# Row sums of a 16384 x 1024 matrix: the last group's loads in other sizes, and another moment for the first store

## The chip, the cores and the metric

The kernel runs on one core of a Trainium2 chip. The metric is the device time of one execution in microseconds (us), the median of several executions. A profile of one execution comes with it: its span starts with the first load that SyncE issues and ends with the closing work of the program.

## The reference

The input x has 32 x 512 rows of 1024 float32 numbers (67.1 MB). The output is the sum of each row.

```python
def reference(x):          # x: (32, 512, 1024) float32
    return np.sum(x, axis=-1).astype(np.float32)
```

## The kernel before

The 16384 rows are cut into 8 groups of 2048. In a group each of the 128 partitions holds 16 consecutive rows (`BIG = 16`), so one group is 8 MB, and 64 KB in each partition. A group lies in a tile `t` of a pool with three buffers; the sums of all rows gather in one tile `sums` of 128 x 128 numbers, 16 columns for each group.

All loads are issued by SyncE, in the order of the program (lines 137 and 179). A load of a group waits until VectorE has read the group that used its buffer before. The order of the work on each engine is that of the program text.

Three helpers add up rows:

- `vec` (line 98) is one VectorE reduction over several rows.
- `act` (line 125) is one ScalarE copy of one row with an accumulated output; its copy goes to a PSUM tile `unread` that nobody reads.
- `halves` (line 112) is a custom VectorE instruction for one row or a part of one: it adds the second half of its input to the first half, element by element, and accumulates the sums. An instruction that reads the accumulator out follows it.

`rows` (line 134) loads `n` rows for each partition and sums them: the first `n - n_act` by `vec`, the last `n_act` by `act`, one after the other.

Groups 0 to 5 are summed by VectorE alone (group 0 is loaded as 4 and 12 rows), group 6 half by each engine. The last group, number 7, is loaded in pieces of 8, 4, 2 and 1 rows, of which ScalarE sums 4, 2, 1 and 1. Its last row comes in three column pieces of 482, 288 and 254 (`pieces`, line 87; loads at line 179). The three lie one behind the other in the tile, but a free column is left before the third and one after it. The sums of the first two pieces are accumulated into these two free columns, and the third `halves` adds up piece and both columns: `whole`, 256 columns.

There are two stores (line 145). The one of groups 0 to 6 (56 KB) is issued by ScalarE's queue, behind its activations, and it is held until the sum over the first piece is done (`front`, line 186). The one of group 7 (8 KB) is issued by SyncE after the last sum. The closing work of the program (reported at line 214) waits for both.

`order_waits` sets the order in which an instruction with several waits makes them.

Of the kernel before, what the change touches and what calls it, by code (L numbers as in the profile page):

```python
# [58 lines left out]
@with_exitstack  # L59
def kernel(  # L60
    ctx: ExitStack,
    tc: tile.TileContext,
    x: bass.AP,
    out: bass.AP,
):
    nc = tc.nc
    nc.at_finalize(issue_first_load_at_entry)
    nc.at_finalize(order_waits)
    fp32 = mybir.dt.float32
    P = 128  # L70
    batch, seq, dim = x.shape
    rows = batch * seq
    J = rows // P
    BIG = 16


    x_g = x.flatten_outer_dims().rearrange("(g p j) d -> g p j d", p=P, j=BIG)
    out_v = out.rearrange("b s -> (b s)").rearrange("(g p j) -> p g j", p=P, j=BIG)

    def rows_from(j, n):  # L80
        return x_g[j // BIG, :, j % BIG : j % BIG + n, :]

    last = J // BIG - 1
    FIRST = 4
    pieces = (482, 288, 254)

    with (
        tc.tile_pool(name="in", bufs=3) as inpool,  # L90
        tc.tile_pool(name="unread", bufs=4, space=bass.MemoryType.PSUM) as upool,
        tc.tile_pool(name="stage", bufs=1) as stpool,
        tc.manual_schedule(),
    ):
        sums = stpool.tile([P, J], fp32)

        def vec(dst, src):
            return nc.vector.tensor_reduce(  # L98
                out=dst, in_=src, axis=mybir.AxisListType.X, op=mybir.AluOpType.add
            )  # L100

        def hold(inst, until, reason):
            tc.add_manual_dep(
                inst.ins,
                until.ins.name,
                mybir.DependencyInfo(mybir.DependencyClass.Sync, mybir.DependencyReason.DATA),
                reason=reason,
            )

        def halves(dst, src):  # L110
            n = src.shape[-1] // 2
            return nc.vector.tensor_tensor_reduce(  # L112
                out=src[:, :n],
                in0=src[:, :n],
                in1=src[:, n:],
                scale=1.0,
                scalar=0.0,
                op0=mybir.AluOpType.add,
                op1=mybir.AluOpType.add,
                accum_out=dst,  # L120
            )

        def act(dst, src, n):
            unread = upool.tile([P, dim], fp32)
            nc.scalar.activation(  # L125
                out=unread[:, :n],
                in_=src,
                func=mybir.ActivationFunctionType.Copy,
                accum_out=dst,
            )  # L130

        sums_of = []

        def rows(t, a, n, j, n_act):
            nv = n - n_act
            block = t[:, a * dim : (a + n) * dim].rearrange("p (n d) -> p n d", d=dim)
            load = nc.sync.dma_start(out=block, in_=rows_from(j, n))  # L137
            if nv:
                sums_of.append(vec(sums[:, j : j + nv], block[:, :nv, :]))
            for q in range(nv, n):  # L140
                act(sums[:, j + q : j + q + 1], block[:, q, :], dim)
            return load

        def store(eng, g0, g1):
            return eng.dma_start(
                out=out_v[:, g0:g1],
                in_=sums[:, g0 * BIG : g1 * BIG].rearrange("p (g j) -> p g j", j=BIG),
            )

        for g in range(last):  # L150
            t = inpool.tile([P, BIG * dim + 4], fp32)
            if g == 0:
                rows(t, 0, FIRST, 0, 0)
                first = sums_of[-1]
                rows(t, FIRST, BIG - FIRST, FIRST, 0)
                continue
            load = rows(t, 0, BIG, g * BIG, BIG // 2 if g == last - 1 else 0)
            if g == 1:
                hold(load, first, "no descriptors of later loads while the first ones start")

        t = inpool.tile([P, BIG * dim + 4], fp32)
        a = 0
        j = last * BIG
        for n, n_act in ((8, 4), (4, 2), (2, 1), (1, 1)):
            rows(t, a, n, j + a, n_act)
            a += n

        j += a
        at = a * dim
        c = 0
        parts = []
        for width in pieces:
            if len(parts) == len(pieces) - 1:
                at += 1
            part = t[:, at : at + width]
            nc.sync.dma_start(out=part, in_=rows_from(j, 1)[:, 0, c : c + width])
            parts.append(part)  # L180
            at += width
            c += width
        whole = t[:, at - width - 1 : at + 1]
        front = halves(whole[:, :1], parts[0])
        halves(whole[:, width + 1 :], parts[1])
        hold(store(nc.scalar, 0, last), front, "its packets come behind those of the loads")
        halves(sums[:, j : j + 1], whole)
        store(nc.sync, last, last + 1)

# [29 lines left out]
```

## Time and profile before

| | |
|---|---|
| median of 4 runs | 163.01 us (162.18 to 163.09) |
| the profiled execution: time | 163.05 us |
| the profiled execution: span | 161.3 us |
| VectorE (DVE) busy | 121.1 us, 75% |
| ScalarE (ACT) busy | 18.5 us, 11% |
| GpSimd (POOL) busy | 0.2 us |
| HBM read over the span | 67.11 MB, 417 GB/s |

In the lines of the profile, PE, DVE, ACT, POOL and SP are TensorE, VectorE, ScalarE, GpSimd and SyncE; a q behind a name is the queue of the engine that issues its instructions. L98 is line 98 of the kernel. `out<-in` names the tile written and the tile read. In a timeline each line has its start and length in us, the engine, the line, the operation and, in brackets, how long the engine had been idle and what ended that. The chain of work that ended last is followed back from the last instruction, at each step to what released it.

### The profile page before, as it was taken

To read this page: it belongs to the slowest core of one execution; us is meant where nothing else is said; L and a number is where in the kernel's file an instruction comes from. 1 tells how busy PE (TensorE), PEld (TensorE's weight loads), DVE (VectorE), ACT (ScalarE), POOL (GpSimd) and SP (SyncE) were. 2 spreads that over 40 slices of the span, in tenths; PEclk is the share of its full clock that TensorE was granted. 3 is DMA by queue.
4 is the path that set the end of the run, shared out by engine and by line. 5 is a ranking of instruction groups with operands and counts; after the bars stand their busy time and mean duration, and the time that the engine had idled before them with its cause. 6 is when DMAs were issued, how large, how long until landed. Compare 5 with 4: busy or idle time off the path is not lost.

```text
span 161.3 us, 125 instructions
## 1 busy us (share of the span) xinstructions
DVE 121.1 (75%) x17; ACT 18.5 (11%) x33; POOL 0.2 (0%) x4
## 2 busy tenths in 40 slices
DVE  0280069960899949999399994999949998597982
ACT  3000000000000000000000000000000000596882
POOL 0000000000000000000000000000000000000000
DMA  7999995996996996979959959959969959999992
GB/s 264 451 524 451 390 520 260 520 520 260 520 520 260 520 520 260 520 309 471 520 260 520 520 260 520 520 260 520 520 260 520 520 260 520 390 390 451 402 400 63
DMA packets 3216, 67.18 MB, mean 417 GB/s; under 512 B 1296, under 2 KB 1680, under 8 KB 1808
## 3 DMA queue, kind: packets, MB, share of 16 engines
q1 hardware_dynamic: 2304, 67.12, 97.4%
q10 hardware_dynamic: 912, 0.06, 0.3%
HBM read 67.11 MB, written 0.07 MB: 417 GB/s over the span
## 4 chain that ended last, share of the span: by engine, by line
DMA 73%; DVE 25%; SPq 1%; issue 0%; DVEq 0%
DMA t<-in_x_dram 73%; DVE sums L98 24%; SPq L137 1%; DVE t L112 1%; DVEq L112 0%; DVEq L214 0%
## 5 line engine op out<-in xcount | busy, mean ns | idle before, releaser
L98 DVE TENSOR_REDUCE sums<-t 128x16 f32<-128x16384 f32 (+5 forms) x11 | 120.1, 10917 | 36.9 <-DMA t<-in_x_dram 36.9
L125 ACT ACTIVATE unread<-t 128x1024 f32<-128x1024 f32 x16 | 16.2, 1013 | 139.0 <-DMA t<-in_x_dram 138.9
L125 ACT ACTIVATION_READ_ACCUMULATOR unread<-t 128x1 f32 x16 | 3.0, 187 | 0.0
L112 DVE CUSTOM_DVE_ANT_0 t<-t 128x241 f32<-128x241 f32 (+2 forms) x3 | 1.0, 338 | 0.9 <-DMA t<-in_x_dram 0.8
L125 ACT ACT_TABLE_LOAD x1 | 1.3, 1283 | 0.8 <-PEq L203 0.8
L112 DVE DVE_READ_ACCUMULATOR2_ANT t<- 128x1 f32 x2 | 0.2, 82 | 0.0
L203 POOL MEMSET const-bfloat16-1.0<- 128x1 bf16 x1 | 0.1, 102 | 0.0
L203 POOL MEMSET const-uint8-127<- 128x1 uint8 x1 | 0.1, 102 | 0.0
L203 POOL MEMSET const-float32-0.0<- 128x1 f32 x1 | 0.1, 99 | 0.2 <-issue 0.2
L203 POOL MEMSET const-float32-1.0<- 128x1 f32 x1 | 0.1, 99 | 0.0
L112 DVE DVE_READ_ACCUMULATOR2_ANT sums<- 128x1 f32 x1 | 0.1, 83 | 0.0
## 6 DMA issues: line engine op xcount, KB each, us to landing
t<-in_x_dram SPq DMA_DIRECT2D x1, 6144.0 KB, 20.9
t<-in_x_dram SPq DMA_DIRECT2D x2, 2048.0 KB, 21.4
t<-in_x_dram SPq DMA_DIRECT2D x1, 4096.0 KB, 31.2
t<-in_x_dram SPq DMA_DIRECT2D x1, 1024.0 KB, 37.7
t<-in_x_dram SPq DMA_DIRECT2D x1, 512.0 KB, 38.5
t<-in_x_dram SPq DMA_DIRECT2D x1, 241.0 KB, 38.7
t<-in_x_dram SPq DMA_DIRECT2D x1, 144.0 KB, 38.6
t<-in_x_dram SPq DMA_DIRECT2D x1, 127.0 KB, 38.4
```

The costliest lines, as they stand in the source:

```text
L98: return nc.vector.tensor_reduce(out=dst, in_=src, axis=mybir.AxisListType.X, op=mybir.AluOpType.add)
L112: return nc.vector.tensor_tensor_reduce(out=src[:, :n], in0=src[:, :n], in1=src[:, n:], scale=1.0, scalar=0.0, op0=mybir.AluOpType.add, op ...
L125: nc.scalar.activation(out=unread[:, :n], in_=src, func=mybir.ActivationFunctionType.Copy, accum_out=dst,)
L137: load = nc.sync.dma_start(out=block, in_=rows_from(j, n))
L203: nc = _bacc.Bacc("TRN2", target_bir_lowering=False, num_devices=1)
```

## The change

The last group is loaded as 8, 5 and 2 rows and then a last row in two column pieces of 560 and 464; before it was 8, 4, 2 and 1 rows and a last row in three pieces. ScalarE sums 4, 2 and 1 rows of the three row loads. In the pieces of 5 and 2 rows, VectorE's rows (3 and 1) are no longer summed by one `vec` but by one `halves` for each row. The second column piece of the last row has one free column ahead of it, which takes the sum of the first piece, and one behind it, which VectorE fills with zero, so that `whole` has an even number of columns (466). The store of groups 0 to 6 is held until the last `halves` of the two-row piece is done, instead of the sum over the first column piece.

```diff
-    pieces = (482, 288, 254)
+    pieces = (560, 464)
...
-        def rows(t, a, n, j, n_act):
+        def rows(t, a, n, j, n_act, pairs=False):
             nv = n - n_act
             block = t[:, a * dim : (a + n) * dim].rearrange("p (n d) -> p n d", d=dim)
             load = nc.sync.dma_start(out=block, in_=rows_from(j, n))
-            if nv:
+            if pairs:
+                for q in range(nv):
+                    sums_of.append(halves(sums[:, j + q : j + q + 1], block[:, q, :]))
+            else:
                 sums_of.append(vec(sums[:, j : j + nv], block[:, :nv, :]))
...
-        a = 0
         j = last * BIG
-        for n, n_act in ((8, 4), (4, 2), (2, 1), (1, 1)):
-            rows(t, a, n, j + a, n_act)
-            a += n
-
+        rows(t, 0, 8, j, 4)
+        rows(t, 8, 5, j + 8, 2, pairs=True)
+        rows(t, 13, 2, j + 13, 1, pairs=True)
+        a = BIG - 1
...
-        at = a * dim
-        c = 0
-        parts = []
-        for width in pieces:
-            if len(parts) == len(pieces) - 1:
-                at += 1
-            part = t[:, at : at + width]
-            nc.sync.dma_start(out=part, in_=rows_from(j, 1)[:, 0, c : c + width])
-            parts.append(part)
-            at += width
-            c += width
-        whole = t[:, at - width - 1 : at + 1]
-        front = halves(whole[:, :1], parts[0])
-        halves(whole[:, width + 1 :], parts[1])
-        hold(store(nc.scalar, 0, last), front, "its packets come behind those of the loads")
+        c, width = pieces
+        whole = t[:, a * dim + c : BIG * dim + 2]
+        nc.vector.memset(whole[:, width + 1 :], 0.0)
+        part = t[:, a * dim : a * dim + c]
+        nc.sync.dma_start(out=part, in_=rows_from(j, 1)[:, 0, :c])
+        nc.sync.dma_start(out=whole[:, 1 : width + 1], in_=rows_from(j, 1)[:, 0, c:])
+        hold(store(nc.scalar, 0, last), sums_of[-1], "its packets come behind those of the loads")
+        halves(whole[:, :1], part)
         halves(sums[:, j : j + 1], whole)
         store(nc.sync, last, last + 1)
```

## The prediction

> **What bounds the kernel now.** I read the page's chain first, then the chain in order of time, then the timeline of the last 13 us, then the busy time by stretches around the end. The chain says who ends last:
>
> ```profile
> DMA t<-in_x_dram 73%; DVE sums L98 24%; SPq L137 1%; DVE t L112 1%; DVEq L112 0%; DVEq L214 0%
> ```
>
> The loads of x are 73% of it, and the 24% of the reductions at line 98 are no second bound: they are stretches in which the chain walks through the reduction that frees a buffer while loads go on beside it (page: 417 GB/s mean over the span). The change lies in the last group only, so its price is read from the end of the chain (start, length, what; all in us):
>
> ```profile
> 119.03 38.72 DMA t<-in_x_dram
> 157.74 0.02 issue
> 157.77 0.69 DVE t L112 x4
> 158.46 0.03 issue
> 158.49 0.02 DVEq L112
> 158.51 0.08 issue
> 158.59 0.29 DVE t L112
> ```
>
> At 157.74 the first piece of the last row has landed. From there VectorE is the chain: two sums over pieces (0.69 with their accumulator reads), then 0.13 in which the third sum waits for the results of the first two, because it reads them, then the third sum, 0.29. The timeline gives landings (an instruction that had waited for a load starts 0.02 after it) and the two stores:
>
> ```profile
> 148.41 4.42 DVE L98 TENSOR_REDUCE sums<-t 128x4 f32<-128x4096 f32 x1 [1.03 <-DMA t<-in_x_dram]
> 153.30 2.29 DVE L98 TENSOR_REDUCE sums<-t 128x2 f32<-128x2048 f32 x1 [0.47 <-DMA t<-in_x_dram]
> 155.79 1.22 DVE L98 TENSOR_REDUCE sums<-t 128x1 f32<-128x1024 f32 x1 [0.20 <-DMA t<-in_x_dram]
> 157.08 1.03 ACT L125 ACTIVATE unread<-t 128x1024 f32<-128x1024 f32 x1
> 158.22 0.42 ACTq L145 DMA_DIRECT2D out_dram<-sums  x1
> 158.92 0.35 SPq L145 DMA_DIRECT2D out_dram<-sums  x1
> ```
>
> The pieces of 8, 4, 2 and 1 rows landed at 148.39, 153.28, 155.77 and 157.06. VectorE stood idle before each (the brackets), so it keeps up with the loads until the last row. The table of DMA issues puts the last piece (127 KB) at 38.4 after an issue at 120.0, so at 158.4, and the stores' landings at 2.1 after 158.22 (160.3) and 1.6 after 158.92 (160.5). The second ends the program; 0.8 of closing work follows it to 161.3. The profiled execution took 163.05: its span plus 1.75 around it. It lies 0.04 above the median of the four runs, 163.01.
>
> **The loads.** Seven loads become five. The four-row piece took 153.28 - 148.39 = 4.89, or 1.22 a row, the two-row piece 2.49, the single row 1.29. Five rows at 1.22 are 6.11, so they land at 154.50, and two rows at 2.49 land at 156.99, where the single row landed at 157.06: 0.07 earlier. If the fifth row keeps the price of the single row (1.29), the gain is nothing. The last row took 158.4 - 157.06 = 1.34 in three pieces and would take 1.29 or a little less as one; for two I take the middle, 1.31. The last landing is then 156.99 + 1.31 = 158.30, with 158.25 and 158.40 as ends. The first of two pieces, 560 columns, has 482 of them priced by the old first piece, 157.74 - 157.06 = 0.68; scaled by 560/482 that is 0.79, so it lands at 157.78.
>
> Against this stands a rule. The Trainium skill, page DMA: Bandwidth & Descriptors, section Anatomy of one DMA, gives each transfer a fixed 2.0 us beside its bytes (fitted on the GpSimd path, while these loads come from SP); two transfers fewer would by that be an estimated 4 us. The trace disagrees: the three pieces land within 1.34 together, so a transfer's fixed part lies beside the others' bytes, and the sum above stands.
>
> SP issues all of these around 117 to 120.5, when 38 us of transfers are queued ahead, so two issues fewer (0.48 each at most) bring nothing. No queue is moved past by them.
>
> **VectorE.** The three sums over halves took 411, 310 and 294 ns for 241, 144 and 128 elements: 160 ns and 1.04 ns for an element. So a whole row (512 elements) is 693, the 560-column piece (280) 452, and the last one (466 columns with the two added ones, 233 elements) 403. One starts 0.05 before its forerunner ends (157.77 + 0.41 against 158.13).
>
> - Eight-row piece: as before, 4.42.
> - Five-row piece, three paired rows: 154.52 + 3 x 0.65 = 156.5, half a microsecond ahead of the next landing. Where the cover is gone (each would have to wait 0.13 as the third sum does), it is 156.9, still before 157.01.
> - Two-row piece: row 13 runs 157.01 to 157.70. Before, ScalarE had this time alone; VectorE waited 0.75. The next instruction may start at 157.66.
> - The new zero fill of one column stands behind it in VectorE's queue. No such fill is in the trace on VectorE; GpSimd's four take 0.10, an accumulator read on VectorE 0.08, and the longest that I allow is a sum's fixed 0.16 with the wait of 0.13. I take 0.10, nearest in kind, so to 157.76: hidden, as the first piece lands at 157.78. At 0.29 it would push the chain by 0.15. Below nothing it can't go, since it is added.
> - First piece: 157.80 to 158.25, accumulator read out at 158.26. The last sum reads that result, so the 0.14 between the read (end 158.45) and the third sum (158.59) stays: 158.40. Its data are there at 158.30, so VectorE, not the load, is last here.
> - Last sum: 158.40 + 0.40 = 158.80, against 158.88 before.
>
> So one link of three in the closing chain goes, but the links that stay are longer and the first comes after a row's sum. Net: 0.08 earlier. With the load's worst end (158.40 + 0.02) it is 0.06; with the slow fill 0.07 later than before.
>
> **ScalarE and the stores.** ScalarE takes seven rows of the group instead of eight; its last one starts at 157.01 instead of 157.08 and ends at 158.16 instead of 158.23. SP's last store waits for that too, hidden by 0.64 of VectorE's work. The store of the first seven groups waited for the first piece (158.18, issued at 158.22). Now it waits for row 13, done at 157.72, and stands on ScalarE's queue behind the last activation. Which of the two holds it the trace doesn't show: 157.75 if the queue runs ahead of the engine, 158.18 if not. Nothing else is queued behind it. Its landing at 2.1 comes to 159.85 or 160.28, before the last store's in both cases, so this step is worth nothing on the path, or up to 0.1 if the last store meets fewer of its packets. Does it hurt the loads? The stretches show (length, busy of the engines, clock, DMA share, GB/s):
>
> ```profile
> 148.40:153.20 4.80, 4.42 (x1) 4.27 (x8) 0.00 (x0) 1.00 0.98 420
> 153.20:155.60 2.40, 2.29 (x1) 2.19 (x4) 0.00 (x0) 1.00 0.97 408
> ...
> 156.60:157.60 1.00, 0.41 (x1) 0.86 (x3) 0.00 (x0) 1.00 1.05 361
> 157.60:158.00 0.40, 0.23 (x1) 0.40 (x1) 0.00 (x0) 1.00 0.44 147
> 158.00:159.00 1.00, 0.75 (x6) 0.23 (x2) 0.00 (x0) 1.00 0.00 0
> 159.00:159.40 0.40, 0.00 (x0) 0.00 (x0) 0.00 (x0) 1.00 0.45 45
> 159.40:160.00 0.60, 0.00 (x0) 0.00 (x0) 0.00 (x0) 1.00 0.77 79
> ```
>
> The loads' bytes end before 158.0, and the stores' bytes begin after 159.0, some 0.8 to 0.9 behind the issue at 158.22. Issued at 157.75, they begin at 158.55 at the earliest: still behind the loads.
>
> **Sum.** 163.05 - 0.08 = 162.97 for the profiled execution; by the median, 163.01 - 0.08 = 162.93, so 162.9. The last store still lands 1.6 after its issue at 158.84.
>
> **The rivals.**
> 1. *The loads gain more.* The rate falls from 420 GB/s in the stretch of the four-row piece to 361 where the single row and the pieces run, and the two-row piece's stretch has 408. If the single row (0.52 MB) moves from 361 to 408, that is 1.45 - 1.29 = 0.16, everything behind it comes earlier, and with up to 0.1 from the last store the time is about 162.7. Against it: the single row's landing came only 1.29 after its forerunner.
> 2. *VectorE becomes later.* The fill and a wait in front of the first piece cost 0.29 and row 13 starts late (157.08): the last sum starts at 158.6 or 158.7 and is longer by 0.11, so 163.1 to 163.2. For it speaks that row 13's sum is new in the last microsecond.
> 3. *Slower: the store's packets get in between the last loads.* Place: the 16 DMA engines at 157 to 158. Price: the stores keep them busy 0.45 x 0.40 + 0.77 x 0.60 = 0.64 in the stretches above, and if all of that goes before the last piece the time is 163.01 - 0.08 + 0.64 = 163.6. It decides from an issue some 0.85 before the loads' last byte, so before about 157.1; the wait for row 13 (157.72) speaks against it, unless the store follows something that is ready sooner than I read. The Trainium skill (same page, section Queues, rings and completion order) says that an engine alternates between queues packet by packet, which would make this the cost of every early store; no load and store overlap in this trace.
> 4. *Nothing that counts changes*: the gain of the loads and the longer last sum cancel (the load's worst end and the fill at 0.29 give 163.1), and the four runs spread from 162.18 to 163.09 anyway.
>
> **How the numbers follow.** About 0.5% (0.82 us) is what a measurement of this kernel can tell from no change. Chances: the forecast 0.50 (162.8 to 163.0), rival 1 0.18, rival 2 0.13, rival 3 0.07, rival 4 0.12. No step that I priced reaches 0.82 in either direction. Faster by more than that needs rival 1 together with a median at the low end of the spread of runs (162.18 is at the line): 0.14. Slower needs rival 3 with its price above the sum, or a wait that the trace doesn't show: 0.09. The rest, 0.77, is within. The range runs from the lowest run of before, 162.2, to rival 2 with half of rival 3, 163.4.
>
> **What would show it.** In the changed profile: the two-row piece's sums start at 157.0; three paired rows of 0.69 end before that; the last sum starts 0.14 behind an accumulator read, not 0.02 behind a landing; SP's store is issued at 158.8 to 158.9; no store bytes before 158.5. I am wrong if the last load lands after 158.5, if the store's bytes appear beside load bytes, if a paired row takes clearly over 0.7, or if the time moves by over 0.5 in either direction.

## The result, and the profile after

The changed kernel takes 162.13 us (median of 54 runs, 161.86 to 162.75), the kernel before, measured with it, 162.51 us (78 runs, 162.10 to 163.12). The ratio is 0.9981, 95% interval 0.9974 to 0.9988: faster by 0.31 us, or 0.20 to 0.42 by the interval, and so within 0.5%. The means, 162.23 and 162.54, differ by that 0.31; the medians lie 0.38 apart, the fastest runs 0.24. The profiled execution took 162.01 with a span of 160.2.

The spans of the two profiled executions differ by 1.04, far more than that. Where the difference lies is seen from the eight-row piece of the last group: its sums start at 148.41 before and at 147.56 after, so 0.85 of it had come up ahead of anything that was changed. It was complete at the sums of group 4 (99.98 against 99.13), long before SyncE issued the first load of the last group (117.2 and 116.4). In the fourteen profiles of this study that start lies between 147.43 and 148.41, as far apart as the runs of one kernel. I therefore call it the mark, and count from it. The landings and ends of spans below are the trace's own time stamps, which the profile's tables round to 0.1; the times of the stores' packets (a packet is one piece of a transfer on one DMA engine) are from the trace's packet records.

The chain of the changed kernel in order of time, its end (start, length, what):

```profile
118.23 39.34 DMA t<-in_x_dram
157.57 0.04 issue
157.62 0.40 DVE t L112
```

The chain now goes over from the loads to VectorE with one sum left, instead of three with a wait in between. The timeline shows what is around it:

```profile
147.56 4.42 DVE L98 TENSOR_REDUCE sums<-t 128x4 f32<-128x4096 f32 x1 [1.03 <-DMA t<-in_x_dram]
153.78 0.69 DVE L112 CUSTOM_DVE_ANT_0 t<-t 128x512 f32<-128x512 f32 x1 [1.80 <-DMA t<-in_x_dram]
156.29 1.03 ACT L125 ACTIVATE unread<-t 128x1024 f32<-128x1024 f32 x1 [0.32 <-DMA t<-in_x_dram]
156.29 0.69 DVE L112 CUSTOM_DVE_ANT_0 t<-t 128x512 f32<-128x512 f32 x1 [0.59 <-DMA t<-in_x_dram]
156.94 0.06 DVE L176 MEMSET t<- 128x1 f32 x1
157.01 0.45 DVE L112 CUSTOM_DVE_ANT_0 t<-t 128x280 f32<-128x280 f32 x1
157.02 0.41 ACTq L148 DMA_DIRECT2D out_dram<-sums  x1
157.39 0.08 DVE L112 DVE_READ_ACCUMULATOR2_ANT t<- 128x1 f32 x1
157.62 0.40 DVE L112 CUSTOM_DVE_ANT_0 t<-t 128x233 f32<-128x233 f32 x1
158.05 0.35 SPq L148 DMA_DIRECT2D out_dram<-sums  x1
```

The last sum ends 10.46 after the mark; before, it ended at 10.47. The closing chain of loads and sums is in this profile no shorter at all. What is shorter stands in the table of DMA issues, as the time from issue to landing of the two stores (KB, us). The first two lines are the changed kernel's, the third is the last store of the kernel before; the first store has 2.1 there too:

```profile
out_dram<-sums ACTq DMA_DIRECT2D x1, 56.0 KB, 2.1
out_dram<-sums SPq DMA_DIRECT2D x1, 8.0 KB, 1.4
out_dram<-sums SPq DMA_DIRECT2D x1, 8.0 KB, 1.6
```

The last store landed 1.6 after its issue before, and 1.4 now. The stretches of the changed kernel say why (length, busy of DVE, ACT, POOL, clock, DMA share, GB/s):

```profile
157.40:157.80 0.40, 0.26 (x3) 0.04 (x1) 0.00 (x0) 1.00 0.00 0
157.80:158.20 0.40, 0.23 (x2) 0.00 (x0) 0.00 (x0) 1.00 0.46 46
158.20:158.60 0.40, 0.00 (x0) 0.00 (x0) 0.00 (x0) 1.00 0.81 85
158.60:158.80 0.20, 0.00 (x0) 0.00 (x0) 0.00 (x0) 1.00 0.29 26
158.80:159.20 0.40, 0.00 (x0) 0.00 (x0) 0.00 (x0) 1.00 0.23 21
```

The first store's bytes begin to move at 157.98, as VectorE ends its last sum, and go on while the last store is only being issued (158.05). They are through at 158.72, and the last store has the engines to itself. In the kernel before the two ran into each other: the first store's packets moved from 159.18 to 159.95, those of the last one from 159.77 to 160.01. The queues' packets in the stretch around the last store's show it (queue: packets, MB, share of 16 engines; q10 is ScalarE's queue, q1 SyncE's). The first two lines are the kernel before, 159.70 to 160.10, the third is the changed kernel, 158.72 to 159.20, where q10 has none:

```profile
q10 hardware_dynamic: 233, 0.01, 34.5%
q1 hardware_dynamic: 144, 0.01, 21.8%
q1 hardware_dynamic: 144, 0.01, 19.3%
```

### The profile page after: what moved, and what is told of

It is laid out like the page before. It is cut to its first block, busy times and chain, and to the rows that moved or that the text cites. A ratio compares the mean times of both kernels' runs of the same rounds, so it can differ in the third digit from the quotient of the medians.

```text
span 160.2 us, 126 instructions
## 1 busy us (share of the span) xinstructions
DVE 120.1 (75%) x22; ACT 17.3 (11%) x31; POOL 0.2 (0%) x4
## 4 chain that ended last, share of the span: by engine, by line
DMA 73%; DVE 25%; SPq 1%; issue 0%; DVEq 0%
DMA t<-in_x_dram 73%; DVE sums L98 24%; SPq L137 1%; SPq L178 0%; DVE t L112 0%; DVEq L209 0%
## 5 line engine op out<-in xcount | busy, mean ns | idle before, releaser
L98 DVE TENSOR_REDUCE sums<-t 128x16 f32<-128x16384 f32 (+3 forms) x9 | 116.6, 12953 | 35.4 <-DMA t<-in_x_dram 35.4
L125 ACT ACTIVATE unread<-t 128x1024 f32<-128x1024 f32 x15 | 15.2, 1012 | 139.4 <-DMA t<-in_x_dram 139.4
L112 DVE CUSTOM_DVE_ANT_0 t<-t 128x512 f32<-128x512 f32 (+2 forms) x6 | 3.5, 603 | 2.5 <-DMA t<-in_x_dram 2.4
```

Of the source, the lines that this page charges most:

```text
L98: return nc.vector.tensor_reduce(out=dst, in_=src, axis=mybir.AxisListType.X, op=mybir.AluOpType.add)
L112: return nc.vector.tensor_tensor_reduce(out=src[:, :n], in0=src[:, :n], in1=src[:, n:], scale=1.0, scalar=0.0, op0=mybir.AluOpType.add, op ...
L125: nc.scalar.activation(out=unread[:, :n], in_=src, func=mybir.ActivationFunctionType.Copy, accum_out=dst,)
```

## The experiments

Each was timed beside the kernel before. The table gathers what the profiles show from the mark on; the two stores of each kernel are called the first (groups 0 to 6, ScalarE's queue) and the last (group 7, SyncE's queue).

| kernel | first store issued | last sum ends | last store lands | landing less last sum | span ends | ratio (95% interval) |
|---|---|---|---|---|---|---|
| before | 9.81 | 10.47 | 12.11 | 1.64 | 12.86 | 1 |
| changed | 9.46 | 10.46 | 11.92 | 1.46 | 12.67 | 0.9981 (0.9974 to 0.9988) |
| changed, again | 9.35 | 10.36 | 11.81 | 1.45 | 12.56 | 0.9981 (0.9966 to 0.9997) |
| changed, store late | 9.83 | 10.35 | 12.12 | 1.77 | 12.87 | 1.0007 (0.9991 to 1.0023) |
| the same, again | 9.94 | 10.45 | 12.23 | 1.78 | 12.98 | 0.9997 (0.9978 to 1.0016) |
| before, store early | 8.68 | 10.48 | 11.93 | 1.45 | 12.68 | 0.9998 (0.9981 to 1.0014) |
| the same, again | 8.69 | 10.50 | 11.95 | 1.45 | 12.70 | 0.9981 (0.9963 to 0.9998) |

**The changed kernel again**, with no edit.

> The changed kernel itself, once more, as the mark for the others. In the first pair of profiles I count from the start of the sums of the eight-row piece (148.41 before, 147.56 changed), since both kernels are alike up to there: the last sum ended 10.48 later before and 10.46 changed, the last store landed after another 1.63 before and 1.46 changed, and the span ended 12.9 and 12.6 after the mark. All theories expect the same here: last sum 10.45 to 10.50 after the mark, last store landing 1.4 after its issue, time 0.2 to 0.4 us under the kernel before.

The last sum ended at 10.36 instead of 10.46, so this part of the tail differs by 0.1 between executions of one kernel; the last store landed 1.4 after its issue, as before. The ratio, 0.9981, is the same.

**The changed kernel with the old moment of the store**, run twice.

```diff
-        hold(store(nc.scalar, 0, last), sums_of[-1], "its packets come behind those of the loads")
-        halves(whole[:, :1], part)
+        front = halves(whole[:, :1], part)
+        hold(store(nc.scalar, 0, last), front, "its packets come behind those of the loads")
```

> The changed kernel, but the store of groups 0 to 6 follows the sum over the first column piece again. Store theory (the gain comes from the last store, which finds the first store's packets gone): the first store is issued at about 157.5 instead of 157.0, its bytes end at about 159.2 instead of 158.7, the last store lands 1.6 instead of 1.4 after its issue, and 0.15 to 0.2 of the gain of 0.31 goes. Load theory (fewer and larger loads bring the end): time as the changed kernel, 0.3 under the kernel before. VectorE theory (a shorter closing chain): also unchanged.

The gain is gone. The last store's landing in its table of DMA issues:

```profile
out_dram<-sums SPq DMA_DIRECT2D x1, 8.0 KB, 1.7
```

The last sum ended 0.12 earlier than in the kernel before, and the last store still landed at the same 12.1 after the mark: what the sums gave, the store took back. In the stretches the store bytes of this kernel end before 159.8, at 11.6 after the mark, as those of the kernel before do (160.0):

```profile
159.40:159.80 0.40, 0.00 (x0) 0.00 (x0) 0.00 (x0) 1.00 0.74 74
159.80:160.00 0.20, 0.00 (x0) 0.00 (x0) 0.00 (x0) 1.00 0.00 0
```

The first store is issued at the same distance from the mark in both (9.81 and 9.83), and it is this that fixes the end. I expected 0.15 to 0.2 of the gain to go; the two runs, 1.0007 and 0.9997 (mean 1.0002), leave nothing of it. The second was expected so:

> The changed kernel with the store after the first column piece, once more (first 1.0007, interval 0.9991 to 1.0023): the new loads and sums without the new moment of the store. If the first store's packets set the end, the shorter closing chain (0.1) is worth nothing alone: last store landing 12.1 after the mark, span end 12.85, ratio 1.000. If loads and sums count by themselves, 12.75 and 0.9993 or less.

Its first store was issued at 9.94 and its last store landed at 12.23. In the three profiles with a late first store of 56 KB (before, and these two) the last store thus landed 2.30, 2.29 and 2.29 after the first one's *issue*, while it came 1.64, 1.77 and 1.78 after the last sum: it is tied to the first store and not to the sum. The two intervals alone would allow 0.9993 too; the landings decide for 1.000.

**The kernel before with an early store**, run twice.

```diff
-        hold(store(nc.scalar, 0, last), front, "its packets come behind those of the loads")
+        hold(store(nc.scalar, 0, last), sums_of[-1], "its packets come behind those of the loads")
```

> The kernel before, but its first store follows the reduction of the two-row piece (done at 157.01 in its profile) instead of the first column piece (158.18). Store theory: issue at about 157.05, store bytes from 157.95, the last store lands 1.4 instead of 1.6 after its issue, and the time falls by 0.15 to 0.2, so half or more of the changed kernel's gain with the old loads. Load and VectorE theories: no gain. If store bytes and the last load meet (the loads' bytes end at about 157.95), the last landing comes up to 0.1 later.

The tail is 0.18 shorter (12.68), all of it between the last sum and the landing of the last store (1.45 instead of 1.64). The times left it open, hence once more:

> The kernel before with its first store behind the two-row piece, once more: the first time its profile showed the tail 0.18 shorter than the kernel before, as the store theory said, but the times (0.9998, interval 0.9981 to 1.0014) told neither 0.9989 nor 1.000 apart. Store theory: last store landing 1.4 after its issue, tail from the mark to the end of the span 12.65 to 12.70 against 12.86, ratio 0.999. Load theory: ratio 1.000.

Tail 12.70, ratio 0.9981. The mean of the two, 0.9990, is the 0.999 of the store theory, but the two differ by more than the effect that is sought, since the part ahead of the mark varies. It is the tails, which agree within 0.02, that decide.

**An earlier store still**, behind the last paired row of the five-row piece.

```diff
-        hold(store(nc.scalar, 0, last), sums_of[-1], "its packets come behind those of the loads")
+        hold(store(nc.scalar, 0, last), sums_of[-2], "its packets come behind those of the loads")
```

> The changed kernel, but the first store follows the last paired row of the five-row piece (done at 155.7) instead of the one of the two-row piece (157.0): this puts the store's bytes at about 156.6 to 157.4, beside the last column piece. My prediction's third rival prices that at up to 0.64. If the packets of the two queues alternate on each engine, the last landing comes 0.3 to 0.6 later than 10.0 after the mark and the time is 0.2 to 0.5 us above the changed kernel; if small stores fit beside loads, the time is as the changed kernel within 0.1.

It missed its aim. The sum it waited for was read out by 155.80, but the timeline has the store at 156.46, just behind the start of ScalarE's last activation, which had waited for the two-row piece:

```profile
156.40 1.03 ACT L125 ACTIVATE unread<-t 128x1024 f32<-128x1024 f32 x1 [0.33 <-DMA t<-in_x_dram]
156.46 0.41 ACTq L148 DMA_DIRECT2D out_dram<-sums  x1
```

So its bytes again came behind the loads (from 9.60 after the mark, where the last load packet ended at 9.47), and the tail (12.53) and the ratio, 0.9981 (0.9963 to 0.9999), are those of the changed kernel. Between issues at 8.67 and 9.46 after the mark nothing is left to gain.

**The store beside the last row's loads.** Here the store also stands ahead of that activation in ScalarE's queue.

```diff
+        hold(store(nc.scalar, 0, last), sums_of[-1], "beside the loads of the last row")
         rows(t, 13, 2, j + 13, 1, pairs=True)
...
-        hold(store(nc.scalar, 0, last), sums_of[-1], "its packets come behind those of the loads")
```

> The changed kernel, but the store of groups 0 to 6 stands ahead of ScalarE's last activation and follows the last paired row of the five-row piece, so that it is issued about 8.1 after the mark instead of 9.35, and its bytes run from 9.0 to 9.7 after the mark, beside the two column pieces of the last row (the earlier try was held by ScalarE's queue at 8.7). Rival 3: the last piece lands 0.3 to 0.6 later than 9.9 to 10.0 after the mark and the span grows by as much, 0.2 to 0.4% in time. If the packets fit beside the loads, the last piece lands at 10.0 and the time is that of the changed kernel.

Now they meet. The last sum, which in the changed kernel follows its forerunner, had to wait for the load:

```profile
157.78 0.40 DVE L112 CUSTOM_DVE_ANT_0 t<-t 128x233 f32<-128x233 f32 x1 [0.33 <-DMA t<-in_x_dram]
```

It starts 10.13 after the mark, against 9.96 and 10.06 in the two profiles of the changed kernel, and the span ends at 12.73, 0.06 to 0.17 later. The ratio, 0.9986 (0.9966 to 1.0005), doesn't tell that from 0.9981. The collision shows in the landings: from the five-row piece to the last column piece it took 4.03, against 3.81 to 3.85 in the seven profiles of these loads in which no store moved beside them. So the last piece landed 0.2 later, and the end came 0.06 to 0.17 later, where the lower end of the expectation was 0.3. It is no full test of that price, since only 300 of the store's 896 packets moved before the last load packet did.

**Both stores together.**

```diff
-        hold(store(nc.scalar, 0, last), sums_of[-1], "its packets come behind those of the loads")
...
-        halves(sums[:, j : j + 1], whole)
+        end = halves(sums[:, j : j + 1], whole)
+        hold(store(nc.scalar, 0, last), end, "its packets come with those of the last store")
```

> The changed kernel, but the store of groups 0 to 6 follows the last sum, so both stores are issued together, about 10.4 after the mark (the start of the eight-row piece's sums). This takes the store's delay to its end. The first store has landed 2.1 after its issue in every profile so far. Store theory: the program now ends with the first store, 2.1 after the last sum instead of 1.4, so the span is 0.65 longer than the changed kernel's and the time about 0.4% above it (ratio to the kernel before about 1.002). If the closing stores did not matter (load or VectorE theory), the time stays at 0.998 of the kernel before.

Both are issued at 10.39; the first lands 2.1 later, at 12.54, and the span ends at 13.42, 0.75 to 0.86 behind the two profiles of the changed kernel. The ratio is 1.0024 (1.0007 to 1.0041), as expected. This is the largest effect of the store's moment, and the clearest in time: with the same loads and sums, the store alone moves the ratio from 0.998 to 1.002. The last store landed 1.47 after its issue here, hardly later than with nothing beside it, though the other store's packets moved beside its own: this time its packets were in front (from 11.27, the other's from 11.38).

**A part of the store in the middle of the loads.** Groups 0 to 5 are stored when group 5 is summed; the store at the old place keeps group 6.

```diff
+            if g == last - 1:
+                hold(store(nc.scalar, 0, g), sums_of[-1], "beside the loads of the last two groups")
             load = rows(t, 0, BIG, g * BIG, BIG // 2 if g == last - 1 else 0)
...
-        hold(store(nc.scalar, 0, last), sums_of[-1], "its packets come behind those of the loads")
+        hold(store(nc.scalar, last - 1, last), sums_of[-1], "its packets come behind those of the loads")
```

> The changed kernel, but groups 0 to 5 are stored by ScalarE's queue as soon as group 5 is summed (about 135.7), in the middle of the loads of groups 6 and 7; group 6 alone is stored where the changed kernel stores groups 0 to 6. Bandwidth reading (rival 3 of my prediction): 48 KB in small packets take 6/7 of 0.64, so everything after comes 0.55 later, and the time is 0.3% above the changed kernel. Reading by alternating packets: each small packet waits for a load's large one, so the store lands only near the end, many microseconds after its issue, but the loads lose little; then the time is that of the changed kernel within 0.1%, or above it if the store's rest meets the last store.

From its table of DMA issues:

```profile
out_dram<-sums ACTq DMA_DIRECT2D x1, 48.0 KB, 22.1
```

22.1 us instead of 2.1: the store was issued at 135.70 and landed at the end of the loads. Its first packet moved at 139.39, beside the eight-row piece. That piece still took 9.71 from the start of the sums before it to the start of its own (137.80 and 147.51; changed kernel 137.84 and 147.56, so 9.72). But from the five-row piece to the last one it took 3.94, 0.1 more than with no store beside, and the last sum ended at 10.51, 0.05 to 0.15 late. The packets of the two queues from 140 to 152 (q1 has the loads, q10 the store):

```profile
q1 hardware_dynamic: 208, 4.92, 95.5%
q10 hardware_dynamic: 208, 0.01, 1.2%
```

One packet of the store for each one in the queue of the loads: the reading by alternating packets holds. The packets of the loads were of 32 and 20 KB there, those of the store of 64 bytes, so the store got on slowly. The Trainium skill (DMA: Bandwidth & Descriptors, section Queues, rings and completion order) has an engine take its queues in turn, packet by packet, and these rows agree. There is nothing to win: 0.9997 (0.9979 to 1.0015).

**A small store at the old moment.** As the one above, but the 8 KB of group 6 follow the first column piece.

```diff
-        hold(store(nc.scalar, last - 1, last), sums_of[-1], "its packets come behind those of the loads")
-        halves(whole[:, :1], part)
+        front = halves(whole[:, :1], part)
+        hold(store(nc.scalar, last - 1, last), front, "its packets come behind those of the loads")
```

> The changed kernel with groups 0 to 5 stored in the middle of the loads, and group 6 alone stored after the sum over the first column piece, the late moment of the kernel before (9.8 after the mark). In the two kernels with a late store of 56 KB the last store landed 12.1 after the mark whether the last sum ended at 10.47 or at 10.35. If it is the first store's number of packets that sets this end, the small late store frees it: the last store lands 1.45 after the last sum and the span ends 12.55 to 12.75 after the mark, as in the changed kernel. If a late store of any size costs it, the span ends at 12.85. Ratio to the kernel before 0.998 or 1.000.

The last store landed 12.06 after the mark, but the last sum had ended late, at 10.62; from sum to landing it is 1.44, as in every kernel with an early store, though this store was issued at 10.05. So it is the number of packets in front, not the mere fact of a second store, that delays the last one: the small store's were through at 11.12, before the last store's began at 11.50. The span, 12.81, missed the expected stretch because the closing loads were late. From the five-row piece to the last one they took 3.94, so 0.1 more, as with the store in the middle above. The five-row piece itself had landed late too (6.25), and the eight-row piece took 9.92. Why stays open: in the next run, which has no store in the middle, these are 6.36 and 9.96. The ratio is 0.9991 (0.9976 to 1.0007).

**No paired sums.**

```diff
-        rows(t, 8, 5, j + 8, 2, pairs=True)
-        rows(t, 13, 2, j + 13, 1, pairs=True)
+        rows(t, 8, 5, j + 8, 2)
+        rows(t, 13, 2, j + 13, 1)
```

> The changed kernel, but VectorE's rows of the five-row and the two-row piece are summed by one reduction each again. All theories: the reduction of three rows takes 3.35 (between 2.29 for two and 4.42 for four) from 6.12 after the mark to 9.5, that of row 13 another 1.22 to 10.7, then the first piece's sum 0.45, a wait of 0.14 and the last sum 0.40: it ends 11.7 after the mark instead of 10.36, so the paired sums carry 1.3 us of the new loads, and the ratio to the kernel before is about 1.006.

The last sum ended at 11.79 (expected 11.7) and the span at 13.99, 1.3 to 1.4 behind the changed kernel. The ratio is 1.0045 (1.0027 to 1.0063), so slower by 0.7 than the kernel before; its upper end takes in the expected 1.006. With one reduction for each row load, the larger loads cost more than they bring; the paired sums carry them.

**The old row loads with two column pieces and the early store.** The end of the changed kernel (line 174 on) is put into the kernel before.

```diff
-    pieces = (482, 288, 254)
+    pieces = (560, 464)
...
-        hold(store(nc.scalar, 0, last), front, "its packets come behind those of the loads")
+        hold(store(nc.scalar, 0, last), sums_of[-1], "its packets come behind those of the loads")
```

> The kernel before with the last row in two column pieces of 560 and 464 and the early store, but with the old row loads (8, 4, 2, 1) and reductions. If the shorter closing chain comes from the column pieces alone, the last sum ends 10.35 to 10.42 after the mark, against 10.48 to 10.50 with three pieces and the early store, and the span 12.55 to 12.62 after it: as good as the changed kernel, ratio 0.998. If the larger row loads bring it, the last sum ends at 10.5 and the span at 12.7, ratio 0.999.

Last sum at 10.45, span at 12.66, ratio 0.9985 (0.9969 to 1.0002). That lies between the two expectations, and inside the spread of the last sums with the new loads (10.33 to 10.46). Whether the row loads or the column pieces bring the last tenth stays open.

## Why the prediction was right, and where it was off

**What held.** Faster, by less than can be told at 0.5%. The number of 162.9 came from four runs with a median of 163.01; with 78 runs it is 162.51, and most of the distance between forecast and measured time is that. For the same reason the measured 162.13 lies just under the 162.2 at which my range begins. As a difference, I said 0.08, and it is 0.31 (0.20 to 0.42). So "faster, and by less than 0.5%" was right, but the sum had only a quarter of the gain; that it stayed within 0.5% all the same is owed to how small both are.

**Loads.** I put the two-row piece's sums at 8.60 after the mark; they started at 8.73 and 8.62 in the two profiles. The five-row piece landed at 6.19 and 6.08, for 6.09 expected, and the last piece at 10.01 and 9.90, for 9.89. These terms had the right size, with a spread of 0.1 that I had not allowed for. The 0.07 that the row loads were to bring can't be told from that spread: the last of them landed 8.58 to 8.71 after the mark in six profiles of the new loads (mean 8.62), and at 8.65 in three of the old ones.

**VectorE.** The durations were right to 0.01: 0.69, 0.45, 0.40. The zero fill took 0.06 instead of 0.10, and the last sum started 0.15 behind the accumulator read, as named. I had VectorE last there; the chain names the load, which landed 0.05 ahead of that sum, so the two are level. With six profiles of the new loads and paired sums in which no store met the closing loads, the last sum ended on average at 10.38, with three of the old ones at 10.48: a gain of 0.10 for the 0.08 of the sum, which had the last sum end at 10.39. The size stands; that the row loads bring it is not shown, as the last experiment says.

**ScalarE and the stores: the step that failed.** I wrote that the first store's earlier landing "is worth nothing on the path, or up to 0.1 if the last store meets fewer of its packets". In the tails it is worth 0.17 with the old loads (12.86 against 12.69, the mean of two) and 0.31 with the new ones (12.93 against 12.62, means of two). I had compared the two landings, 160.3 and 160.5, and concluded that the first was off the path because it came first. But the last store's bytes were among the first one's, and its landing time carried that: 1.6 instead of 1.4. The row that I used as a fixed price was itself a sum. That the packets in front cause it, the small late store shows. Where it arises can be read from the packet records. In ten profiles no other store's packets met those of the last store: its last packet ended 1.05 after its issue, and the landing followed 0.36 to 0.38 behind that. In the kernel before it was 1.09 and 0.51, in the two runs of the changed kernel with the late store 1.23 to 1.24 and 0.51. So 0.14 of the delay comes after the last packet, and in all three of these profiles the last store landed 0.17 behind the first one; the rest, 0.04 before and 0.19 in the other two, comes while the packets wait and move. A smaller misreading changed nothing: I had the first bytes of ScalarE's store 0.8 to 0.9 behind its issue, and by the packet records they come 0.96 behind it (159.18).

**The same step hid a second thing.** In the kernel before, the end of both stores' bytes was set by the first store's issue. So the 0.08 that I had for loads and sums would by itself have brought nothing: with them and the late store the ratio is 1.0002 (mean of two). The two parts together give 12.86 - 12.62 (mean of the changed kernel's two tails) = 0.24, of the 0.31 measured.

**The rivals.** Rival 1 (the loads gain more) had the size but named the loads for it; only its last term, the store, was right, and too small. Rival 2's late VectorE didn't come. Rival 3's collision didn't come in the changed kernel, whose store bytes begin at 10.42 after the mark, 0.8 behind the last load packet. Where it was brought about, it cost the last piece 0.2 with a third of the store in front of the loads' end, and 0.1 with a part of it in the middle of the loads; 0.64 was nowhere seen.

## What to carry to other kernels

A transfer that lands before the last one can still be what the last one waits behind: look at whether their bytes overlap, not only at which landing comes last. The chain of waits doesn't show it, because no instruction waits for it. Before shortening a closing chain, compare the last store's time from issue to landing with that of the same store with nothing in front of it; if it is longer, move the other store first. In this kernel the gain of the chain was lost otherwise.

## What the runs showed of the hardware

- ScalarE's queue issues a store while the activation in front of it still runs (0.06 behind the start of one of 1.03), but not while that activation waits for its load: the sum that it was held for had been read out 0.66 earlier. I had left open whether it waits for the end.
- A store of 48 KB in packets of 64 bytes beside loads in larger packets landed after 22.1 us instead of the 2.1 that 56 KB take alone. Beside load packets of 32 and 20 KB it moved one packet for each of theirs (208 and 208); the eight-row piece beside it took no longer (9.71 against 9.72), and the closing loads came 0.1 later.
- The last store landed 0.37 behind its last packet when no other store's packets were in front of its own, and 0.51 behind it when they were.
- The spread between executions (162.1 to 163.1 for the kernel before) arises ahead of the last group: the mark moved by 1.0 between the profiles, while the tails of one kernel agreed within 0.02 to 0.11.
